# Splitting the last 512-column matrix product ahead of a run of 256-column ones into two halves (two transformer blocks, one Trainium2 core)

## The chip, the cores and the metric

The kernel runs on one core of one Trainium2 chip. The metric is the device time of one execution in microseconds (us). A matrix product here is one TensorE instruction pair: a weight load, which puts a 128x128 stationary operand into the array, and a product, which streams 256 or 512 columns of a second operand past it and adds into a bank of PSUM.

## The reference

Two transformer blocks in sequence on 256 tokens of width 1024, all in float32. Cut to what matters here:

```python
# first block (context tokens feed only the mixer's state)
h = modulate(rmsnorm(x, g0), sh1, sc1)
x = x + g1 * hgrn2_mixer(hc, h, hg_w_in, ...)       # q, f_fwd, f_bwd, i, g = h @ w_in ; ... @ hg_w_out
u = dwconv(modulate(rmsnorm(x, g1_), sh2, sc2) @ ffn_w_up, conv_w, conv_b)   # 1024 -> 2*2816
gate, val = split(u); x = x + g2 * ((silu(gate) * val) @ ffn_w_down)         # 2816 -> 1024
x = rmsnorm(x, final_g)
# second block
proj = rmsnorm(x, pre_mix_norm) @ w_in               # retention, windowed attention, two gates
merged = sigmoid(gate_r) * (ret @ w_ret_out) + sigmoid(gate_s) * (swa @ w_swa_out)
x = x + rmsnorm(merged @ w_out, post_mix_norm)
u = square(relu(rmsnorm(x, pre_mlp_norm) @ w_up))    # 1024 -> 4096
x = x + rmsnorm(u @ w_down, post_mlp_norm)           # 4096 -> 1024
```

## The kernel before

Every large matrix product is taken as three. Each float32 operand is split into a high part (rounded to the type that TensorE streams in one pass) and a low rest, and `mm3` adds high*high, high*low and low*high into one PSUM bank: line 345, 346 and 347, in this order. The weights come from memory in halves of 128x1024 (512 KB) and are split on the core into tiles `hi` (ScalarE, line 157) and `lo` (VectorE, line 158). The activations stand in `hT` (high and low part, transposed, the contraction on the partitions).

The products come in two widths, and the kernel alternates between them.

- **256 columns, into `x` (or `m`) banks.** `fm_product` takes one chunk of 256 output features. The weight slice is loaded as the stationary operand, and 256 tokens of `hT` stream past it: 2 feature halves x 8 contraction steps x 3 = 48 products. In a row of the trace such a product reads `x<-hT,hi` or `x<-hT,lo`: out, then what streams, then what is loaded.
- **512 columns, into `m` banks.** `row_product` multiplies the activations of 256 features back to 1024 output columns. Here the activation is loaded (`ah`, `al`: its high and low part) and 512 columns of weight stream past: `m<-hi,ah`, `m<-lo,ah`, `m<-hi,al`. Its function `go(j)` issues 2 contraction steps x 2 token halves x 2 column halves x 3 = 24 products, into four banks `acc[0..3]` that are kept open over all j.

`row_product` is used four times: for `o1` (the mixer's output, n = 4 chunks), `dn` (the first block's down projection, n = 11), `o2` (the second mixer's output, n = 4) and `d2` (the second down projection, n = 16). `go(j)` covers the first n - SKEW chunks (SKEW = 3), one between two groups of `fm_product`; `finish` takes the last three chunks in another order, one bank after the other. In the first block's feed-forward stage a period is two `fm_product` (gate and value, 96 products) and one `go`; in the second's it is one `fm_product` (48 products) and one `go`.

Other shapes that the prediction reads: the value projection of the first mixer (`v_half`) has the roles turned, weights stream and `hT` is loaded (`m<-hi,hT`, 256 columns); the products with `w_swa_out` stream the split attention output `swh`, `swl` (`x<-swh,hi`, 24 products in a row); `mm3_rows` (lines 331, 335, 336) loads `hT` and streams weights. The start of the program has products of 512 columns with `hT` streaming (`f0_mm`, into four banks `zf`), and the query chunk's 256-column products follow them.

The order on each engine is written out in the kernel; nothing is scheduled by a compiler, and TensorE takes its instructions in that order.

Of the kernel before, what the change touches and what calls it, by code (L numbers as in the profile page):

```python
# [17 lines left out]
KT = 8  # L18
# [12 lines left out]
SKEW = 3  # L31
# [21 lines left out]
def kernel(ctx: ExitStack, tc: tile.TileContext, a, out):  # L53
    nc = tc.nc
    v_, s_, g_, t_ = nc.vector, nc.scalar, nc.gpsimd, nc.tensor
# [8 lines left out]
    def bank(tag):  # L64
        return ps.tile([128, 512], F32, tag=tag, name=tag, bufs=4)
# [103 lines left out]
    def use(i, keep=None, ahead=None):  # L169

        assert i == at_["u"], (i, at_["u"])
        at_["u"] += 1
        at_["rel"] = chunks[i if keep is None else keep][0]
        a0, a1 = chunks[i]
        pump(len(halves) if ahead is None else a1 + ahead)
        assert at_["s"] >= a1
        w = []
        for j in range(a0, a1):
            r = ready.pop(j)
            for k in range(halves[j][1] if r else 0):  # L180
                w.append((r[0][:, k, :], None if r[1] is None else r[1][:, k, :]))
        return w
# [5 lines left out]
    def part_done(i):  # L188

        at_["rel"] = max(at_["rel"], chunks[i][0] + 1)  # L190
        pump(len(halves))
# [103 lines left out]
    start = ctx.enter_context(ExitStack())  # L295
# [43 lines left out]
        for k in range(KT - n, KT):  # L339
            lo(k)  # L340

    def mm3(o, w, x, start, stop):
        wh, wl = w
        xh, xl = x
        t_.matmul(o, wh, xh, start=start, stop=False)  # L345
        t_.matmul(o, wh, xl, start=False, stop=False)  # L346
        t_.matmul(o, wl, xh, start=False, stop=stop)  # L347

    oTs = res.tile([128, 4, 512], F32, name="oTs")

# [8 lines left out]
    def hT(k, c0, c1):  # L359
        return hTh[:, k, c0:c1], hTl[:, k, c0:c1]  # L360
# [3 lines left out]
    def tick(n=1):  # L364
        for _ in range(n):
            if side:
                side.pop(0)()
# [8 lines left out]
    def fm_product(chunk, nk=KT, x=None, tag="x", ticks=0):  # L376

        w = use(chunk)
        z = bank(tag)
        x = x or (lambda k: hT(k, 0, T))  # L380
        for i in range(2):
            c = slice(i * 128, i * 128 + 128)
            for k in range(nk):
                mm3(z[:, i * T:(i + 1) * T], (w[k][0][:, c], w[k][1][:, c]), x(k), k == 0, k == nk - 1)
                if i and nk == KT and k == KT // 2 - 1:
                    part_done(chunk)
                if ticks and k % 4 == 3:
                    tick(ticks)
        return z
# [45 lines left out]
    def f0_mm(w, k, es):  # L435
        wh, wl = w[0]
        for e in es:
            c = slice(e * 128, e * 128 + 128)
            mm3(zf[e], (wh[:, c], wl[:, c]), hT(k, 0, 512), k == 0, k == KT - 1)

    rs, hs, ar = {}, {}, {}
    cs = const.tile([128, 16], F32, name="cs")
# [25 lines left out]
    for k in range(KT):  # L468
# [5 lines left out]
        if k % 2:  # L474
            v_.tensor_add(sq[k], sq[k - 1], sq[k])
            for i in range(4):
                t_.matmul(sb[:, i * 128:(i + 1) * 128], sq[k][:, i * 128:(i + 1) * 128], ones, start=False,
                          stop=k == KT - 1 and i == 3)
# [13 lines left out]
    for i in range(4):  # L492
        t_.matmul(rb[i // 2][:, i % 2 * 128:i % 2 * 128 + 128], r[:, i:i + 1].to_broadcast([128, 128]), ident,
                  start=True, stop=True)
# [7 lines left out]
    zf = [bank("m") for _ in range(4)]  # L502
# [3 lines left out]
    for k in range(KT):  # L506
        w = use(C["f0", k], ahead=0)
        if k:
            f0_mm(w, k, (0,))
        else:  # L510
            wh, wl = w[0]
            c = [slice(e * 128, e * 128 + 128) for e in range(4)]
            for e in range(4):
                t_.matmul(zf[e], wh[:, c[e]], hTh[:, 0, :], start=True, stop=False)
                t_.matmul(zf[e], wl[:, c[e]], hTh[:, 0, :], start=False, stop=False)
# [11 lines left out]
        if k == 0:  # L527
            nc.scalar.dma_start(hmask, a["hmask"])
            for e in range(4):
                t_.matmul(zf[e], wh[:, c[e]], hTl[:, 0, :], start=False, stop=False)  # L530
        else:
            f0_mm(w, k, (1, 2, 3))
# [201 lines left out]
    for p in range(4):  # L734
# [6 lines left out]
        if p == 0:  # L741
            for e in range(4):
                sigmoid_of(e, zf[e])
        else:
            for d in range(2):
                i = C["ff" if d == 0 else "fb", p]
                w = use(i)
                for hh in range(2):
                    z = bank("m")
                    c = slice(hh * 128, hh * 128 + 128)  # L750
                    for k in range(KT):
                        mm3(z, (w[k][0][:, c], w[k][1][:, c]), hT(k, 0, 512), k == 0, k == KT - 1)
                        if hh and k == 3:
                            part_done(i)
                        if d and k % 4 == 3:
                            tick(2)
                    sigmoid_of(2 * d + hh, z)
                for _ in range(1 + d if p < 3 else 2 * d):
                    ada_step()
# [8 lines left out]
        for d in range(2):  # L768
            kk_[d] = yk.tile([128, 2, 2, T], F32, tag="k", name="k")
            for hh in range(2):  # L770
                e = 2 * d + hh
# [101 lines left out]
        while any(live):  # L873
# [4 lines left out]
            if nstep in v_steps[p]:  # L878
                half = v_steps[p].index(nstep)
# [16 lines left out]
    def splits_to(i):  # L896
        at_["cap"] = i
        pump(len(halves))
# [33 lines left out]
    def row_product(name, n, lhs, done):  # L932

        acc = []

        def mms(j, w, kk, tok, half):
            c = slice(half * 512, half * 512 + 512)
            mm3(acc[2 * tok + half], lhs(j, kk, tok), (w[kk][0][:, c], w[kk][1][:, c]),  # L940
                j == 0 and kk == 0, j == n - 1 and kk == 1)

        def go(j, ticks=0):
            if not acc:
                acc.extend(bank("m") for _ in range(4))
            w = use(C[name, j])
            for kk in range(2):
                for tok in range(2):
                    for half in range(2):
                        mms(j, w, kk, tok, half)  # L950
                    tick(ticks)
                if kk == 0:
                    part_done(C[name, j])

        def finish(*limits, caps=()):
            tail = range(n - SKEW, n)
            w = {}
            for j in tail:
                w[j] = use(C[name, j], keep=C[name, n - SKEW])
                for kk in range(2):  # L960
                    for half in range(2):
                        mms(j, w[j], kk, 0, half)
            d0, d1 = done(0, acc[0:2]), done(1, acc[2:4])
            for i in range(4):
                f0 = next(d0)
                if caps:
                    splits_to(caps[i])
            for j in tail:
                for kk in range(2):
                    mms(j, w[j], kk, 1, 0)  # L970
            next(d1)
            for j in tail:
                if f0 and j == n - 1 - bool(caps):
                    f0()
                    at_["cap"] = 1 << 30
                    pump(limits[0])
                for kk in range(2):
                    mms(j, w[j], kk, 1, 1)
                    at_["rel"] = chunks[C[name, j]][0] + kk + 1
            for limit in limits[1:]:  # L980
                pump(limit, True)
            for _ in limits[1:]:
                next(d1)
                if held:
                    held.pop(0)()
            while held:
                held.pop(0)()
            return [x for x in d1][-1]
        return go, finish
# [231 lines left out]
    w = {}  # L1221
    for tok in range(2):
        for j in range(2):
# [5 lines left out]
            def done(k):  # L1229
                if tok and k % 2:  # L1230
                    at_["rel"] = chunks[C["vr", j, 0]][0] + k // 2 + 1
                    pump(len(halves))
# [325 lines left out]
```

## Time and profile before

| | |
|---|---|
| device time, median of 3 runs | 861.56 us (860.24 to 861.66) |
| device time of the profiled execution | 861.0 us |
| its span in the trace | 859.2 us |
| TensorE busy (products) | 845.5 us, 98% of the span, 6270 products |
| VectorE busy | 603.3 us, 70% |
| ScalarE busy | 488.7 us, 57% |
| mean granted TensorE clock | 0.996 |
| DMA | 161.89 MB, mean 188 GB/s |

The profiled execution's own time is 1.8 us more than its span: what lies ahead of the first and behind the last instruction. A product's row in the trace has a start and a duration. Products overlap, so the duration (0.28 us for 256 columns) is not what one costs; the cost in a run of products is the distance from one start to the next.

### The profile page before, as it was taken

What the parts mean: (1) busy time and instruction counts of PE and PEld (TensorE: products, weight loads), DVE (VectorE), ACT (ScalarE), POOL (GpSimd) and SP (SyncE); (2) the same over time, 40 slices, a digit from 0 to 9 for tenths busy, and PEclk for the clock granted to TensorE, in tenths of its full rate; (3) what the DMA queues carried; (4) which work ended last, traced back from release to release, by engine and by line L of the source; (5) the groups of instructions that cost most, each with busy time, mean ns of one, the idle gap of its engine ahead of it and who ended that gap; (6) DMA issues with size and microseconds to landing.
All of it is one profiled execution on the core that took longest, in us unless ns stands there. A gap on an engine that the chain in (4) does not pass through costs nothing.

```text
span 859.2 us, 15573 instructions
## 1 busy us (share of the span) xinstructions
PE 845.5 (98%) x6270; PEld 773.4 (90%) x6270; DVE 603.3 (70%) x979; ACT 488.7 (57%) x797; POOL 17.1 (2%) x27
## 2 busy tenths in 40 slices
PE   8999999999999999999999999999999999999997
PEld 7798988989987999999988899999999899999995
DVE  5768869877978689887778556665576786555532
ACT  4586575758765575664555546765643674444431
POOL 0000000000000000000000000000000000000000
PEclk9999999999999999999999999999999999999999
DMA  9981735728255667867754654545795188666401
GB/s 350 391 275 49 240 130 158 258 75 269 81 165 184 234 221 243 273 216 223 247 152 99 203 170 145 150 124 172 215 304 169 37 306 253 188 187 189 142 1 49
DMA packets 115784, 161.89 MB, mean 188 GB/s; under 512 B 13952, under 2 KB 95744, under 8 KB 115712
## 3 DMA queue, kind: packets, MB, share of 16 engines
q1 hardware_dynamic: 113408, 155.80, 56.1%
q10 hardware_dynamic: 2304, 5.10, 1.8%
q8 instruction: 49, 0.80, 0.4%
q14 instruction: 23, 0.19, 0.1%
HBM read 159.83 MB, written 1.05 MB: 187 GB/s over the span
## 4 chain that ended last, share of the span: by engine, by line
PE 82%; DVE 9%; ACT 4%; DMA 2%; issue 2%; POOL 0%; POOLq 0%; DVEq 0%; ACTq 0%
PE m L345 15%; PE m L346 15%; PE m L347 15%; PE x L345 8%; PE x L346 8%; PE x L347 8%; DVE lo L158 2%; PE x L712 1%; ACT hi L157 1%; PE x L405 1%; PE x L335 1%; DMA raw<-in_hg_w_in_dram 1%; PE x L336 1%; ACT sig L779 1%; ACT k L774 1%
## 5 line engine op out<-in xcount | busy, mean ns | idle before, releaser
L158 DVE TENSOR_TENSOR lo<-raw,hi 128x1024 fp32r<-128x1024 f32 (+1 forms) x248 | 291.1, 1204 | 127.5 <-ACT hi L157 123.5
L157 ACT ACTIVATE hi<-raw 128x1024 fp32r<-128x1024 f32 (+1 forms) x248 | 249.7, 1040 | 120.4 <-PE x L346 47.6
L345 PE MATMUL m<-hT,hi 128*128 128x256 f32 (+1 forms) x556 | 174.8, 314 | 0.0
L347 PE MATMUL m<-hT,lo 128*128 128x256 f32 (+1 forms) x556 | 168.6, 303 | 0.0
L346 PE MATMUL m<-hT,hi 128*128 128x256 f32 (+1 forms) x556 | 168.5, 303 | 0.0
L345 PE MATMUL x<-hT,hi 128*128 128x256 f32 x592 | 166.4, 281 | 0.0
L346 PE MATMUL x<-hT,hi 128*128 128x256 f32 x592 | 165.7, 280 | 0.0
L347 PE MATMUL x<-hT,lo 128*128 128x256 f32 x592 | 165.7, 280 | 0.0
L345 PEld LDWEIGHTS m<-hT,hi 128*128 128x128 f32 x556 | 104.5, 188 | 9.5 <-issue 4.4
L347 PEld LDWEIGHTS x<-hT,lo 128*128 128x128 f32 x592 | 113.0, 191 | 0.0
L345 PEld LDWEIGHTS x<-hT,hi 128*128 128x128 f32 x592 | 111.3, 188 | 1.0 <-ACT hi L157 0.2
L346 PEld LDWEIGHTS x<-hT,hi 128*128 128x128 f32 x592 | 111.1, 188 | 1.0 <-issue 0.2
L346 PEld LDWEIGHTS m<-hT,hi 128*128 128x128 f32 x556 | 104.6, 188 | 5.4 <-DVE hT L433 0.7
L347 PEld LDWEIGHTS m<-hT,lo 128*128 128x128 f32 x556 | 104.3, 188 | 5.1
L345 PE MATMUL m<-hi,ah 128*128 128x512 f32 x248 | 96.7, 390 | 0.0
L347 PE MATMUL m<-hi,al 128*128 128x512 f32 x248 | 96.6, 390 | 0.0
L346 PE MATMUL m<-lo,ah 128*128 128x512 f32 x248 | 96.5, 389 | 0.0
L347 PEld LDWEIGHTS m<-hi,al 128*128 128x128 f32 x248 | 46.6, 188 | 9.9 <-DVE al L1198 0.2
L346 PEld LDWEIGHTS m<-lo,ah 128*128 128x128 f32 x248 | 46.6, 188 | 8.7
L345 PEld LDWEIGHTS m<-hi,ah 128*128 128x128 f32 x248 | 46.6, 188 | 8.6
L591 DVE SCALAR_TENSOR_TENSOR vr<-raw,cs,vr 128x1024 f32<-128x1024 f32 x28 | 35.8, 1280 | 0.4
L345 PE MATMUL m<-hi,hT 128*128 128x256 f32 x128 | 35.8, 280 | 0.0
(314 smaller groups left out, 1237.2 us busy)
## 6 DMA issues: line engine op xcount, KB each, us to landing
raw<-in_ffn_w_up_dram SPq DMA_DIRECT2D x44, 512.0 KB, 5.2
raw<-in_w_in_dram SPq DMA_DIRECT2D x42, 512.0 KB, 4.1
raw<-in_hg_w_in_dram SPq DMA_DIRECT2D x36, 512.0 KB, 5.2
raw<-in_w_ada_dram SPq DMA_DIRECT2D x32, 512.0 KB, 5.6
raw<-in_w_up_dram SPq DMA_DIRECT2D x32, 512.0 KB, 4.8
raw<-in_w_down_dram SPq DMA_DIRECT2D x32, 512.0 KB, 3.7
raw<-in_ffn_w_down_dram SPq DMA_DIRECT2D x22, 512.0 KB, 4.4
ar<-in_ada_dram SPq DMA_DIRECT2D x16, 512.0 KB, 7.7
```

The source lines that it names most:

```text
L157: s_.activation(h[:, :w], r[:, :w], AF.Copy)
L158: held.append(lambda r=r, h=h, l=l, w=w: v_.tensor_tensor(l[:, :w], r[:, :w], h[:, :w].bitcast(F32), op=OP.subtract))
L335: t_.matmul(o, hTh[:, k, c], w[k][0], start=k == 0, stop=False)
L336: t_.matmul(o, hTh[:, k, c], w[k][1], start=False, stop=False)
L345: t_.matmul(o, wh, xh, start=start, stop=False)
L346: t_.matmul(o, wh, xl, start=False, stop=False)
L347: t_.matmul(o, wl, xh, start=False, stop=stop)
L405: t_.matmul(rw[g, :256], c2[:, kk, :], ar[k][kk // 4][:, kk % 4, :], start=kk < 4, stop=kk >= 4)
L591: v_.scalar_tensor_tensor(acc, w[kk][0], cs[:, k:k + 1], acc, op0=OP.mult, op1=OP.add)
L712: t_.matmul(z[:, b * 128:(b + 1) * 128], l, r, start=i == 0, stop=i == len(terms) - 1)
L774: s_.activation(kk_[d][:, :, hh, :], sig[e], AF.Identity, scale=noml[:, ix:ix + 1], bias=oml[:, ix:ix + 1])
L779: s_.activation(sig[e], sig[e], AF.Ln, scale=oml[:, ix:ix + 1], bias=lb[:, ix:ix + 1])
```

## The change

`mm3` gets a flag. Where it is set, the third product (low part loaded, high part streamed) is issued as two products of 256 columns, into the two halves of the same bank, each with its own load of the same stationary operand. The flag is set for the last product of `f0_mm` and, in `row_product`, for the last product of every `go(j)` and for the last product of `finish`.

```diff
-    def mm3(o, w, x, start, stop):
+    def mm3(o, w, x, start, stop, halved=False):
+
+
         wh, wl = w
         xh, xl = x
         t_.matmul(o, wh, xh, start=start, stop=False)
         t_.matmul(o, wh, xl, start=False, stop=False)
-        t_.matmul(o, wl, xh, start=False, stop=stop)
+        if halved:
+            t_.matmul(o[:, 0:256], wl, xh[:, 0:256], start=False, stop=False)
+            t_.matmul(o[:, 256:512], wl, xh[:, 256:512], start=False, stop=stop)
+        else:
+            t_.matmul(o, wl, xh, start=False, stop=stop)
...
-            mm3(zf[e], (wh[:, c], wl[:, c]), hT(k, 0, 512), k == 0, k == KT - 1)
+            mm3(zf[e], (wh[:, c], wl[:, c]), hT(k, 0, 512), k == 0, k == KT - 1, e == 3 and k == KT - 1)
...
             mm3(acc[2 * tok + half], lhs(j, kk, tok), (w[kk][0][:, c], w[kk][1][:, c]),
-                j == 0 and kk == 0, j == n - 1 and kk == 1)
+                j == 0 and kk == 0, j == n - 1 and kk == 1,
+                kk and tok and half and (j < n - SKEW or j == n - 1))
```

TensorE then has 28 more products: one at `f0`, two at `o1`, nine at `dn`, two at `o2` and fourteen at `d2`. The other engines' instructions stay in number and order. Behind 20 of the 28 places a run of `fm_product` with `hT` streaming follows at once (7 at `dn`, 1 at `o2`, 12 at `d2`). Behind the others stand the query chunk (`f0`), transposes or `mm3_rows` (`o1`, and `finish` of `o2`), products of 512 columns (the last `go` and `finish` of `dn`, the last `go` of `d2`), and the end of the program (`finish` of `d2`).

On TensorE, the end of one `go` of `d2` and the start of the next `fm_product` stood like this before the change (numbers are line numbers of the kernel before):

```order
L346 MATMUL m<-lo,ah 128x512
L347 MATMUL m<-hi,al 128x512
L345 MATMUL m<-hi,ah 128x512
L346 MATMUL m<-lo,ah 128x512
L347 MATMUL m<-hi,al 128x512
L345 MATMUL x<-hT,hi 128x256
L346 MATMUL x<-hT,hi 128x256
```

The same place with the change (its line numbers are those of the changed kernel, where 347, 348, 353 are the three products and 350, 351 the two halves):

```order
L348 MATMUL m<-lo,ah 128x512
L353 MATMUL m<-hi,al 128x512
L347 MATMUL m<-hi,ah 128x512
L348 MATMUL m<-lo,ah 128x512
L350 MATMUL m<-hi,al 128x256
L351 MATMUL m<-hi,al 128x256
L347 MATMUL x<-hT,hi 128x256
L348 MATMUL x<-hT,hi 128x256
```

The step from 512 to 256 columns now falls one product earlier, within the `m<-hi,al` products, and the step from `hi` streaming to `hT` streaming falls between two products of 256 columns.

At the end of `f0` on TensorE, ahead of the query chunk, `hT` streams on both sides of the step, with the change:

```order
L347 MATMUL m<-hT,hi 128x512
L348 MATMUL m<-hT,hi 128x512
L350 MATMUL m<-hT,lo 128x256
L351 MATMUL m<-hT,lo 128x256
L347 MATMUL m<-hT,hi 128x256
```

Only the width changes there, one product earlier than before; what streams and what is loaded stay of one kind.

## Rows read from the trace of the kernel before

**Rows 1.** The profile's page: span, and shares of the chain that ended last.

```profile
span 859.2 us, 15573 instructions
...
PE 82%; DVE 9%; ACT 4%; DMA 2%; issue 2%; POOL 0%; POOLq 0%; DVEq 0%; ACTq 0%
```

**Rows 2.** Windows, all engines: stretch, length; busy us and count by engine; clock; DMA.

```profile
core 0: us, PE busy (x) PEld busy (x) DVE busy (x) ACT busy (x) POOL busy (x), PEclk, DMA share, GB/s
368.44:385.19 16.75, 16.75 (x121) 15.81 (x120) 12.90 (x18) 10.91 (x14) 0.00 (x0) 1.00 0.68 220
781.15:792.24 11.09, 11.09 (x73) 10.16 (x72) 6.10 (x7) 5.25 (x6) 0.00 (x0) 1.00 0.60 189
```

**Rows 3.** Timeline of TensorE where a go ends: start, duration, instruction.

```profile
703.27 0.39 PE L347 MATMUL m<-hi,al 128*128 128x512 f32 x1
703.50 0.28 PE L345 MATMUL x<-hT,hi 128*128 128x256 f32 x1
703.61 0.28 PE L346 MATMUL x<-hT,hi 128*128 128x256 f32 x1
703.73 0.28 PE L347 MATMUL x<-hT,lo 128*128 128x256 f32 x1
```

**Rows 4.** Windows, TensorE's products with hT: length, busy (count), clock, DMA.

```profile
core 0: us, PE busy (x), PEclk, DMA share, GB/s
296.54:312.75 16.21, 16.21 (x144) 1.00 0.50 158
318.20:329.51 11.31, 11.31 (x96) 1.00 0.80 266
418.68:429.99 11.31, 11.31 (x96) 1.00 0.72 234
638.36:644.02 5.66, 5.66 (x48) 1.00 0.74 228
703.50:709.15 5.65, 5.65 (x48) 1.00 0.61 195
825.52:831.18 5.66, 5.66 (x48) 1.00 0.00 0
```

**Rows 5.** Windows, TensorE: two runs of go, of 24 products each.

```profile
698.04:703.50 5.46, 5.46 (x27) 1.00 0.89 326
709.15:714.59 5.44, 5.44 (x26) 1.00 0.89 276
```

**Rows 6.** Timeline of TensorE where the swh products end.

```profile
646.77 0.28 PE L347 MATMUL x<-swh,lo 128*128 128x256 f32 x1
646.89 0.29 PE L345 MATMUL x<-hT,hi 128*128 128x256 f32 x1
647.01 0.28 PE L346 MATMUL x<-hT,hi 128*128 128x256 f32 x1
647.13 0.28 PE L347 MATMUL x<-hT,lo 128*128 128x256 f32 x1
647.25 0.28 PE L345 MATMUL x<-hT,hi 128*128 128x256 f32 x1
647.36 0.28 PE L346 MATMUL x<-hT,hi 128*128 128x256 f32 x1
```

**Rows 7.** Windows, TensorE's products with hT, behind two runs of swh products.

```profile
624.94:630.03 5.09, 5.09 (x47) 1.00 1.04 372
647.25:652.35 5.10, 5.10 (x47) 1.00 0.55 166
```

**Rows 8.** Windows, TensorE: 21 products of a run with swh and swl.

```profile
644.37:646.89 2.52, 2.52 (x24) 1.00 0.74 222
```

**Rows 9.** Windows, products with hT: the query chunk behind f0, then v_half.

```profile
49.23:54.89 5.66, 5.66 (x49) 1.00 0.80 252
55.36:60.80 5.44, 5.44 (x51) 1.00 0.94 315
```

**Rows 10.** Windows, products with hT: mm3_rows behind finish of o1 and of o2.

```profile
272.35:277.88 5.53, 5.53 (x47) 1.00 0.32 96
672.46:677.79 5.33, 5.33 (x47) 1.00 0.00 0
```

**Rows 11.** Timeline of TensorE behind the first mm3_rows: [idle before <-releaser].

```profile
280.75 0.44 PE L1013 MATMUL x<-ident,ep 128*128 128x128 f32 x2 [2.59 <-DVE ep L1043]
```

## The prediction

> **What bounds the kernel now.** The page's chain first: 82% of it is TensorE [rows 1]. The change touches TensorE alone, so the question is whether TensorE is the bound where the change acts. The windows of one period of each feed-forward stage say yes: of 16.75 us and of 11.09 us TensorE is busy all the time at a granted clock of 1.00 (its upper level, 2.4 GHz), while VectorE is busy 12.90 and 6.10 us, ScalarE 10.91 and 5.25 us, and the DMA engines 68% and 60% [rows 2]. A nanosecond off TensorE's stream there is one off the end, until some 20% have gone.
>
> Next, what a product costs there, from starts and not from durations. A go has 24 products of 512 columns: 5.44 us, 227 ns each [rows 5]. Behind it the products of 256 columns come at 0.11 to 0.12 us from the first one on [rows 3], and the windows resolve it: 96 in 11.31 us, 48 in 5.65 us, which is **117.8 ns** each [rows 4]. The reader should set beside this the first row of that group: the same function, the same shape, also with hT streaming, but behind transposes and not behind a go: 143 products (a window also counts the one to three products that began ahead of it and still drain; this one counts 144) in 16.21 us, **113.4 ns** each, at the same clock. And a third spacing: the products with swh take 2.52 us for 21, **120.0 ns** each [rows 8]. So one shape has three spacings, at full clock, with no wait named in between, and each holds to the end of its series. A series' spacing is set by how it is entered. I call them close (113), wide (118) and widest (120). The rows don't tell what in the engine remembers it.
>
> How many series are wide: behind the go of dn seven of 96 products, the first and the last of them in [rows 4] (318.20, 418.68), both 11.31 us; behind the go of o2 one of 48 (638.36); behind the go of d2 twelve of 48, first and last at 703.50 and 825.52. Those are the 20 places where the change puts its halves ahead of fm_product.
>
> **The change part by part.**
>
> *The halves.* 28 times one product of 227 ns becomes two of 256 columns. At the wide spacing a pair is 235.6 ns, 9 ns more: 28 x 9 = 0.25 us. Bounds: at the close spacing twice 113.4 is 227, nothing; at the widest 240 ns, 0.37 us. I take 0.25, since a series entered from a go is wide from its first product [rows 3]. No wait is added: both halves go to a bank that is open anyway. The last pair (end of d2) adds its 9 ns to the tail, the pair at o1's finish stands ahead of a series behind which TensorE waits 2.59 us for VectorE anyway [rows 11], so it costs nothing; both are inside the 0.25.
>
> *The entry into the series of 256.* Now the width, what streams and what is loaded all change at one step. With the change the width changes first, among products that stream hi, and then the operands change between two products of 256 columns. The trace has that second step elsewhere: from 256 columns of swh to 256 columns of hT. There four starts take 0.47 us (646.89 to 647.36) [rows 6], and then the series is close: 45 products in 5.10 us, 113.3 ns each, and the same behind the swh series before it, 5.09 us [rows 7]. Another change of operands at 256 columns, from the wide query chunk (48 products in 5.66 us) to v_half, also ends in the close spacing (48 products in 5.44 us) [rows 9]. So wherever the operands change between products of 256 columns and hT is streamed or loaded next, the spacing behind is close; I know three such places and they agree. If it holds at the 20 places:
> - at dn a series goes from 11.31 to 96 x 113.3 = 10.88 us: 0.43 x 7 = 3.0 us;
> - at o2 and d2 from 5.65 to 5.44 us: 0.21 x 13 = 2.7 us;
> - the entry itself: 0.47 us against 4 x 113.3 = 0.453, 0.02 us each, 0.4 us in all (bounds: nothing, if the halves have taken it already; 0.4);
> - the next go: behind a close series it took 5.46 us, behind a wide one 5.44 [rows 5], 0.02 x 20 = 0.4 us (bounds 0 and 0.4).
>
> Gain 5.7, cost 0.25 + 0.4 + 0.4 = 1.05, net **4.7 us**.
>
> *The other places.* At f0 hT streams on both sides and only the width changes; nothing there resembles the swh step, so I leave the query chunk wide (if it went close: 5.66 to 5.44, 0.2 us). Behind finish of o1 mm3_rows is wide (47 in 5.53 us), but TensorE waits behind it [rows 10, 11], so a closer series would only wait longer. Behind finish of o2 it is close already, 47 in 5.33 us [rows 10]: nothing to win. That last one is also a warning: it is a step from 512 columns straight into a close series, so the step of width alone doesn't make a series wide.
>
> *Sum.* 861.0 us (the profiled execution's own time) - 4.7 = 856.3. The median of the runs is 0.56 higher, which would make 856.9; I forecast **856.5 us**.
>
> **The rivals.**
>
> *No change of spacing (time 861.8).* The first half of a 512-column product streams what the new half streams, with the same operand loaded next, and the go runs at its steady 227 ns. Then the halves may run at 113.4 as that half does, and hT's first product meets TensorE exactly as it does today, and the series is wide. For it: today all 20 series behind a go come out wide, whatever buffers they use, so what a go leaves behind is very regular. Against it: swh's series at the widest spacing streams the same way as the halves would (a split operand against a split weight), and it does not stay with TensorE when hT follows. Price: the halves alone, 861.56 + 0.25 = 861.8, between 861.4 and 862.2 with the bounds and the runs' spread. The same time comes out if a product of a shape simply has one price and the spacings of [rows 4] have causes elsewhere, such as the operands' places. The Trainium skill, "TensorE: Matmul & The Clock Gate", section "Back-to-back issue gap", gives such a price: N/2.4 + 2.5 ns for an isolated product, 109 ns at 256 columns and 216 at 512, with which the 28 pairs would cost an estimated 0.07 us and no series would change. The trace does not agree with it: at a clock of 1.00 the shape costs 113, 118 or 120 ns.
>
> *Only one of the two stages changes (time 859).* The series of dn are 96 long and those of d2 48, with other buffers loaded. Only dn: 3.0 less 0.25 and about a third of 0.8, 2.5 us; only o2 and d2: 2.7 - 0.25 - 0.5 = 1.9 us. So 858.5 to 859.7. Against it: today they behave alike.
>
> *The halves bring on the widest spacing (time 864.5; the other side).* If two halves start the 120.0 ns of the swh series, and hT's series behind keeps it, 7 x 96 + 13 x 48 = 1296 products cost 2.2 ns more: 2.9 us, with 0.25 for the halves 861.56 + 3.1 = 864.7. It decides the sign alone, and is measurable once more than half of these series keep that spacing. For it: the swh series keep it for 21 products [rows 8]. Against it: no series with hT in the trace does; both that follow swh leave it within three products.
>
> *Another engine takes over.* Close series would shorten dn's period to 16.35 us against 12.90 of VectorE, and d2's to 10.9 against 6.10; the DMA share rises from 68% to 70%. It would need one of them to be at its end, and none is [rows 2]. I give it nothing of its own.
>
> **How the numbers follow.** All or nearly all 20 series close: 0.62. One stage only: 0.06. No change of spacing: 0.26. Widest spacing: 0.06. The forecast is the first case's; its own range, with all costs at nothing (861.0 - 5.7 = 855.3) and all at their upper bounds from the highest of the three times (861.66 - 5.7 + 1.2 = 857.2), is 855.2 to 857.3. To leave out no more than 2 in 10 the range has to reach the case without a change, up to 862.0; below I add 0.2 for the query chunk: 855.0 to 862.0. What this kernel's runs can tell from no change is about 0.2%, 1.7 us. Faster than that: the first two cases, 0.67. Within it: 0.27. Slower: 0.06.
>
> **What would show it right or wrong.** In the changed kernel's windows: the series behind each go of dn at 10.9 us and of d2 at 5.44 to 5.46 (right), 11.3 and 5.65 (no change of spacing), 11.5 and 5.76 (widest). The two halves: starts 0.23 to 0.24 us over the pair. The go behind a close series: 5.46 us. The first three products of hT behind the halves at 0.12 and then 0.113. TensorE still busy through the whole period; if gaps appear in it, with VectorE or a DMA named as what ended them, the bound has moved. The forecast is wrong in its main step if the series stay at 117.8 though the operands now change at 256 columns; then what the three agreeing places share is something else than that.

## The result and the profile after

The changed kernel takes **854.64 us** (854.23 to 854.88, 4 runs) against 861.61 us (860.24 to 861.69, 4 runs): ratio **0.9927**, interval 0.9913 to 0.9941. The forecast was 856.5, with a range of 855.0 to 862.0: faster, as forecast, and by 7.0 us (0.7%) where the sum said 4.7. The time itself lies 0.4 us below the lower end of the range. The profiled execution took 854.23 us.

The page of the changed kernel, its first lines and its chain, beside [rows 1]:

```profile
span 852.4 us, 15630 instructions
...
PE 839.3 (98%) x6298; PEld 767.6 (90%) x6298; DVE 603.1 (71%) x979; ACT 489.2 (57%) x797; POOL 17.1 (2%) x27
...
PE 87%; DVE 6%; ACT 3%; DMA 2%; issue 1%; POOL 0%; SPq 0%; POOLq 0%; DVEq 0%; ACTq 0%
```

28 products more, and TensorE is busy 6.2 us less (845.5 before). Nothing took its place: its share of the chain rose. Windows over one period of `dn` and one of `d2`, all engines (columns as in [rows 2]):

```profile
360.18:376.54 16.36, 16.36 (x123) 15.45 (x122) 13.68 (x21) 9.13 (x12) 0.00 (x0) 1.00 0.78 265
780.68:791.60 10.92, 10.92 (x75) 10.01 (x74) 6.10 (x7) 5.26 (x6) 0.00 (x0) 1.00 0.69 202
```

The periods were 16.75 and 11.09 us. TensorE fills the new ones too. Windows on the series of `hT` behind the go of `dn` (first and last), of `o2`, and of `d2` (first and last), which answer to [rows 4]:

```profile
316.57:327.46 10.89, 10.89 (x96) 1.00 0.80 273
414.73:425.62 10.89, 10.89 (x96) 1.00 0.75 251
633.84:639.30 5.46, 5.46 (x48) 1.00 0.69 207
698.78:704.24 5.46, 5.46 (x48) 1.00 0.59 193
818.90:824.36 5.46, 5.46 (x48) 1.00 0.02 3
```

The other 15 take 10.89 to 10.90 and 5.46 us in the same trace: all 20 series are close. Windows on a go of `d2` with its pair of halves, the first and the second, beside [rows 5]: 

```profile
693.32:698.78 5.46, 5.46 (x27) 1.00 0.87 319
704.24:709.70 5.46, 5.46 (x27) 1.00 0.90 264
```

The timeline of TensorE at the end of that first go, which answers to [rows 3] and reads like [rows 6]:

```profile
698.33 0.39 PE L348 MATMUL m<-lo,ah 128*128 128x512 f32 x1
698.55 0.28 PE L350 MATMUL m<-hi,al 128*128 128x256 f32 x1
698.66 0.28 PE L351 MATMUL m<-hi,al 128*128 128x256 f32 x1
698.78 0.29 PE L347 MATMUL x<-hT,hi 128*128 128x256 f32 x1
698.90 0.28 PE L348 MATMUL x<-hT,hi 128*128 128x256 f32 x1
699.03 0.28 PE L353 MATMUL x<-hT,lo 128*128 128x256 f32 x1
699.14 0.28 PE L347 MATMUL x<-hT,hi 128*128 128x256 f32 x1
```

The pair takes 0.23 us, the first four steps of `hT` 0.48 us (the fifth product starts at 699.26), and from there on the products come at 0.113.

**Where the 6.8 us of span went**, from the starts of the same products in both traces: 0.1 us up to o1's wait at 278 us; **1.5** between there and 296 us; **2.7** over the seven periods of `dn`; 0.4 in the series behind the last go of `dn`, 0.2 of which is given back up to 490 us; 0.2 at `o2`; **2.1** at `d2`. What the sum priced is 2.7 + 0.2 + 2.1 = 5.0. The other 1.5 us lies where the change does nothing: these are windows on TensorE there, first before, then after:

```profile
281.60:296.20 14.60, 14.23 (x110) 0.88 0.65 227
```

```profile
281.60:296.20 14.60, 14.23 (x123) 1.00 0.72 246
```

Before, the granted clock stood below its upper level (2.4 GHz) for some microseconds, right behind the 2.59 us in which TensorE waits for VectorE [rows 11]; products of 256 columns came there at 0.21 us (282.71, 282.92, 283.13). After, the same wait (2.57 us) is followed by a clock of 1.00. Two questions for experiments: is it the break that makes the series close, and does the 1.5 us belong to the change?

### The profile page after: what moved, and what is told of

Its sections match the earlier page's. It is cut to its first block, busy times and chain, and to the rows that moved or that the text cites. A ratio compares the mean times of both kernels' runs of the same rounds, so it can differ in the third digit from the quotient of the medians.

```text
span 852.4 us, 15630 instructions
## 1 busy us (share of the span) xinstructions
PE 839.3 (98%) x6298; PEld 767.6 (90%) x6298; DVE 603.1 (71%) x979; ACT 489.2 (57%) x797; POOL 17.1 (2%) x27
## 4 chain that ended last, share of the span: by engine, by line
PE 87%; DVE 6%; ACT 3%; DMA 2%; issue 1%; POOL 0%; SPq 0%; POOLq 0%; DVEq 0%; ACTq 0%
PE m L347 17%; PE m L348 16%; PE m L353 16%; PE x L353 8%; PE x L347 8%; PE x L348 8%; PE x L718 2%; DVE lo L158 2%; DMA ar<-in_ada_dram 1%; DMA xT<-in_xcT_dram 1%; PE x L648 1%; ACT hi L157 1%; PE x L335 1%; PE x L411 1%; PE x L336 1%
## 5 line engine op out<-in xcount | busy, mean ns | idle before, releaser
L158 DVE TENSOR_TENSOR lo<-raw,hi 128x1024 fp32r<-128x1024 f32 (+1 forms) x248 | 291.0, 1203 | 121.2 <-ACT hi L157 118.9
L347 PE MATMUL x<-hT,hi 128*128 128x256 f32 x592 | 164.3, 278 | 0.0
L348 PE MATMUL x<-hT,hi 128*128 128x256 f32 x592 | 163.6, 276 | 0.0
L353 PE MATMUL x<-hT,lo 128*128 128x256 f32 x592 | 163.5, 276 | 0.0
L353 PEld LDWEIGHTS x<-hT,lo 128*128 128x128 f32 x592 | 111.2, 188 | 0.0
L353 PE MATMUL m<-hi,al 128*128 128x512 f32 x223 | 87.0, 390 | 0.0
L353 PEld LDWEIGHTS m<-hi,al 128*128 128x128 f32 x223 | 41.9, 188 | 9.2 <-DVE al L1205 0.4
```

Source lines behind the costliest of these rows:

```text
L158: held.append(lambda r=r, h=h, l=l, w=w: v_.tensor_tensor(l[:, :w], r[:, :w], h[:, :w].bitcast(F32), op=OP.subtract))
```

## The experiments

Diffs are against the changed kernel unless the text says otherwise. The times of the kernel before that stand beside a run were taken on the same chip as that run.

**1. The halves six products earlier.** 23 go have the broken product as the one that is followed by six of 512 columns; `f0` and the `finish` calls have none.

```diff
-                kk and tok and half and (j < n - SKEW or j == n - 1))
+                kk and not tok and half and j < n - SKEW)
```

> The halves stand six products earlier: in each of the 23 go it is the low*high product of the first token half, second column half, second contraction step, and six products of 512 columns follow it, so that hT follows 512 columns as in the kernel before. Theory (the spacing behind a go is reset because the operands change between two products of 256 columns): the series behind stay wide, 11.31 us per 96 and 5.65 us per 48, and the time is that of before plus 23 x 6 to 9 ns, 861.7 to 861.9 us. Rival (any pair of halves near the end of a go disturbs a regular pattern, and that is enough): the series are close, 10.9 and 5.45 us, and the time is near 857 us.

861.89 us, one execution; before on this chip 861.1 (13 executions, 859.59 to 862.11). Windows on the series of `dn` and `d2`:

```profile
318.14:329.45 11.31, 11.30 (x96) 1.00 0.75 252
704.00:709.65 5.65, 5.65 (x48) 1.00 0.65 199
```

All 20 are wide. A break anywhere near the end of the go is not enough.

**2. Three products earlier.**

```diff
-                kk and tok and half and (j < n - SKEW or j == n - 1))
+                kk and tok and not half and j < n - SKEW)
```

> The halves stand three products earlier: the low*high product of the second token half, first column half, second contraction step of each of the 23 go, with three products of 512 columns behind it. In the trace before, the first products of 512 columns behind a change took 231 to 236 ns and settled to 227 after three to five. Theory (the operands have to change between products of 256 columns): the series stay wide, 861.7 to 861.9 us. Rival (what counts is whether the products just ahead of hT are at their settled 227 ns or still disturbed, as they were ahead of the close series behind finish of o2): the three products behind the halves are at 230 ns or more and the series are close, near 857 us.

862.84 us, one execution. The timeline of TensorE, then a window on the series of `dn` behind it:

```profile
316.83 0.28 PE L350 MATMUL m<-hi,al 128*128 128x256 f32 x1
316.94 0.28 PE L351 MATMUL m<-hi,al 128*128 128x256 f32 x1
317.06 0.40 PE L347 MATMUL m<-hi,ah 128*128 128x512 f32 x1
317.30 0.40 PE L348 MATMUL m<-lo,ah 128*128 128x512 f32 x1
317.53 0.39 PE L353 MATMUL m<-hi,al 128*128 128x512 f32 x1
317.76 0.28 PE L347 MATMUL x<-hT,hi 128*128 128x256 f32 x1
```

```profile
317.76:329.06 11.30, 11.30 (x96) 1.00 0.77 254
```

The first two products of 512 behind the halves take 0.235 us each instead of 0.227, so the go is not at rest when `hT` comes, and yet the series is wide: 96 in 11.30 us. That a disturbed stream is what counts falls. A go with its halves takes 5.51 us here on the mean of 19, against 5.44 before, which is some 1.5 us over 23 go. Another 0.7 us of the loss (862.84 against 861.1) may have nothing to do with the halves: the 156 products of 256 columns with `hT` behind 489 us, in a stretch that no edit touches, take 18.38 us in this trace and 17.70 in that of the kernel before.

**3 and 4. One stage alone.** In experiment 3 the flag is set in `dn` alone (nine places; this is the diff shown), in experiment 4 in `o2` and `d2` (16 places).

```diff
-                kk and tok and half and (j < n - SKEW or j == n - 1))
+                name == "dn" and kk and tok and half and (j < n - SKEW or j == n - 1))
```

> The halves at dn alone, 9 of the 28 places. By the changed kernel's trace a period of dn is 16.36 us against 16.75, seven of them. Theory: -2.7 us, with the halves' cost at the two other places +0.01. If the 1.5 us that the trace gained between 282 and 296 us (a fallen clock in the trace before, none in the one after) comes with the change at o1, it is missing here: 858.9 us. If it is chance from run to run, the time is 858.9 or 857.4 with the granted clock of each run telling which.

> The halves at o2 and d2 alone, 16 of the 28 places. By the changed kernel's trace a period of d2 is 10.92 us against 11.09, twelve of them, and o2 gains 0.19. Theory: -2.3 us, 859.3 us. All of the code up to 632 us is that of the kernel before, so if the fall of the clock at 282 us belongs to that code it is here too, with a mean granted clock of 0.996; if it is chance, some of these runs have 0.998 and are 1.5 us shorter.

`dn` alone: 858.05 us (856.31 to 858.45, 5 executions), ratio 0.996 (0.9946 to 0.9975). `o2` and `d2` alone: 858.54 (857.15 to 858.97, 9), ratio 0.997 (0.996 to 0.998). Windows on a series of `dn` and one of `d2`, in the kernel with `dn` alone and then in the other:

```profile
317.95:328.85 10.90, 10.90 (x96) 1.00 0.73 245
700.69:706.35 5.66, 5.66 (x48) 1.00 0.64 193
```

```profile
316.33:327.64 11.31, 11.31 (x96) 1.00 0.79 260
701.74:707.20 5.46, 5.46 (x48) 1.00 0.64 202
```

Each part turns its own series and leaves those of the other part as they were, and each pays. At a like mean clock `dn` brings 3.0 to 3.2 us (858.2 against 861.2 at 0.997, 856.4 against 859.6 at 0.999) and the other part 2.4 to 2.5 (857.2 against 859.6, 858.7 at 0.996 against 861.2); one of its nine executions, 858.54 us at 0.999, does not fit this split. The 0.4 us that `dn` has over the 2.7 stands behind its last go, whose last product is broken too. There `hT` does not follow at once: two products of 512 columns with `ones` (the trace counts them as four, 1.3 us) stand between. That series of `hT` took 11.71 us before (436.76 to 448.47) and takes 11.30 with `dn` alone (433.79 to 445.09) and with the whole change; it stays at 11.71 in experiment 6, where this one product is whole and the seven before it are broken. Windows on it, with the whole change and in experiment 6:

```profile
432.40:443.70 11.30, 11.30 (x96) 1.00 0.62 182
```

```profile
433.73:445.44 11.71, 11.71 (x96) 1.00 0.59 174
```

So the broken product need not stand right ahead of `hT`.

**5 and 6. The changed kernel again, and only the 20 places in front of a series.** Experiment 6 drops the eight places behind which the diff puts no series:

```diff
-                kk and tok and half and (j < n - SKEW or j == n - 1))
+                kk and tok and half and name != "o1" and j < n - SKEW - (name in ("dn", "d2")))
```

> The changed kernel once more, for how often the granted clock falls behind the wait at 278 to 281 us. In the 13 executions of the kernel before on this chip 11 had a mean clock of 0.997 and about 861.2 us, two 0.999 and 859.6. If the fall is chance, some executions of the changed kernel have it too: 856.2 us at 0.996 to 0.997 and 854.6 at 0.998 to 0.999, and like against like the change is worth 5.0 us. If the change itself keeps the clock up, all executions are near 854.6.

> The halves only at the 20 places ahead of fm_product; left whole again at f0, at both places of o1, at the last go and finish of dn, at finish of o2 and at the last go and finish of d2. In the changed kernel's trace a pair takes 113 + 119 ns against 227, 5 to 6 ns more, so the eight others cost 0.05 us, and finish of o2 had turned the series behind it from close to wide (0.2 us, ahead of a wait). Theory: the gain is all at the 20 places; 854.5 to 854.7 us at the same clock, not to be told from the changed kernel. Rival (one of the eight does something, such as f0 or o1 keeping the clock up): 856 us.

On this chip: before 861.0 (859.33 to 862.08, 17 executions); the change again 854.97 (854.27 to 856.08, 5), ratio 0.9934 (0.9922 to 0.9946); the 20 places 855.96 (854.5 to 857.09, 6), ratio 0.994 (0.9928 to 0.9951). The 20 places have two executions at 854.5, like the change, and four at a lower mean clock between 855.9 and 857.1. The same split runs through before: five of its 17 executions here take 859.3 to 859.8 us, at a mean clock of 0.999; the other twelve take 860.4 to 862.1, eleven of them at 0.996 to 0.998. And one execution of the unaltered change, too, took 856.08 at 0.996. Another execution of the change, 855.79 us at 1.000, is not explained by the clock. So by the mean clocks the fall comes with each of the kernels, in before's more often than not, and the traces agree: over 281 to 283 us the clock is 0.50 with the 20 places and 1.00 in experiment 4, which leaves everything up to 632 us as it was before. The median of the 20 places is the number that I had put down for the rival, but its four longer executions have the lower clock and its two others take what the change takes. The medians therefore can't tell the eight places apart from nothing.

**7 and 8. The wait behind o1 filled.** Nine products of constants into an unused bank go in where TensorE waits, in the kernel before (7) and in the changed kernel (8); nothing reads what they write. The trace counts them as 18.

```diff
+                    if n == 3:
+                        fz = bank("m")
+                        for _ in range(9):
+                            t_.matmul(fz[:, 0:128], ones, ones, start=True, stop=True)
```

> The kernel before, with nine products of 128x128 constants into a free bank put into TensorE's wait of 2.6 us at 278 us; their result is not used. They take about 2 us, less than the wait. If the 1.5 us between 282 and 296 us is the clock that falls behind this wait, all executions are at 859.6 us with 0.999; if the wait has nothing to do with it, most stay at 861.2 with 0.997; if the products are longer than the wait, the time grows by the difference.

> The changed kernel with the same nine products in the wait. Theory: 854.5 us in all executions, and against the kernel before with the products 5.0 us less, which is the change alone with the clock taken out of the comparison.

Timeline of TensorE, filled kernel before, which answers to [rows 11], and the windows there:

```profile
277.69 2.17 PE L1112 MATMUL m<-ones 128*128 128x128 f32 x18
280.41 1.09 PE L1013 MATMUL x<-ident,ep 128*128 128x128 f32 x8 [0.55 <-DVE ep L1043]
281.26 0.36 PE L335 MATMUL x<-hi,hT 128*128 128x256 f32 x1
281.46 0.28 PE L336 MATMUL x<-lo,hT 128*128 128x256 f32 x1
```

```profile
281.60:296.20 14.60, 14.23 (x123) 1.00 0.78 265
```

Before, filled: **859.41** us (859.22 to 859.88, 11 executions), ratio 0.9985 (0.9976 to 0.9993). After, filled: **854.62** (854.29 to 854.91, 5), ratio 0.9927 (0.9915 to 0.9939). With the wait filled no execution of either shows a time or a mean clock of the fall, and before's spread shrinks from 2.8 us to 0.7. Before gains 1.6 us by it, after only 0.35 against its median on this chip. The change by itself is 859.41 - 854.62 = **4.8 us**.

**9 and 10. Broken, but not in halves.** The 28 last products as 128 and 384 columns, then as 384 and 128.

```diff
-            t_.matmul(o[:, 0:256], wl, xh[:, 0:256], start=False, stop=False)
-            t_.matmul(o[:, 256:512], wl, xh[:, 256:512], start=False, stop=stop)
+            t_.matmul(o[:, 0:128], wl, xh[:, 0:128], start=False, stop=False)
+            t_.matmul(o[:, 128:512], wl, xh[:, 128:512], start=False, stop=stop)
```

> As the change, but the product is taken as 128 + 384 columns in place of 256 + 256, at all 28 places: there is a break, but the product just ahead of hT is longer than 256. Theory (the product ahead of hT has to be as short as hT's own): the series behind stay wide, 117.8 ns. Rival (any break of that product in two is enough): close, 113.4 ns. The pair costs about 111 + 170 ns against 227, 55 ns more, 1.5 us in all: 862.7 us if wide, 857.9 if close, at the usual clock of the kernel before.

> The 28 last products are taken as 384 and then 128 columns. If any break of that product into two parts right ahead of hT's products is enough, the 20 series behind it are at 113.3 ns a product, and the time is that of the 128 + 384 kernel, 857 to 858.5 us with the clock fallen behind the 2.6 us wait and 1.5 us less without. If the first part has to be short (at most 256 columns, so that the operand is loaded again at least 109 ns behind the last load), the series stay at 117.8 ns and the time is 861.5 to 863 us, before's with 28 pairs that cost 10 to 60 ns more each. The pair itself: starts 0.23 to 0.29 us over it, as the 286 ns of 128 + 384.

128 + 384: 857.84 us, one execution, before there 861.6. 384 + 128: 855.65, one execution, before there 860.45. The timeline of 128 + 384:

```profile
318.08 0.22 PE L350 MATMUL m<-hi,al 128*128 128x128 f32 x1
318.14 0.39 PE L351 MATMUL m<-hi,al 128*128 128x384 f32 x1
318.37 0.28 PE L347 MATMUL x<-hT,hi 128*128 128x256 f32 x1
318.49 0.28 PE L348 MATMUL x<-hT,hi 128*128 128x256 f32 x1
```

A window on its series of `dn`:

```profile
318.37:329.27 10.90, 10.90 (x96) 1.00 0.80 259
```

With 384 + 128, the first two products of `hT` and a window on the series:

```profile
316.76 0.33 PE L347 MATMUL x<-hT,hi 128*128 128x256 f32 x1
316.93 0.28 PE L348 MATMUL x<-hT,hi 128*128 128x256 f32 x1
```

```profile
316.76:327.72 10.96, 10.96 (x96) 1.00 0.79 257
```

Both are close, with a dearer entry: the pair of 128 + 384 takes 0.29 us, and behind 384 + 128 the first step of `hT` takes 0.17. This fells what I had expected of the first of the two, that the product ahead must be no wider than `hT`'s. At the 20 places its width does not decide; that the go's last product comes in two does. Every cut also loads the same operand twice, and no run separates this second load from the shorter product. Behind the last go of `dn`, where the two products with `ones` stand between, the cuts differ: 11.31 us for 384 + 128 (433.02 to 444.33), but 11.70, wide, for 128 + 384 (434.63 to 446.33).

**11 and 12. The place of `hT`** (against the kernel before). The buffer of `hT` from o1 on is moved by 64 bytes (11); the places of `hT` in the first mixer and from o1 on are swapped, 128 bytes apart (12).

```diff
-    hTh, hTl = h_at(0)
+    hTh, hTl = h_at(16)
```

> The kernel before with no halves, and with hT moved by 64 bytes in its tile from the o1 stage on, so that its rows start at odd multiples of 64 bytes as those of hi, lo, swh and swl do (before, hT's start at multiples of 128 bytes). Asked: whether the spacings hang on the operands' places. If they do, hT's series should act as the swh series, at 120.0 ns whatever stands ahead: some 1900 products of 256 columns with hT streaming behind 296 us go from 113.4 or 117.8 to 120.0, and the time rises by 5 to 9 us, to 866 to 870. If places mean nothing, all spacings and the time (861) stay.

> The kernel before with hT's two places swapped: in its tile hT stands 128 bytes into it up to the g products and at its start from the o1 stage on; here the other way round. Asked: whether the first mixer's series of 256 columns, of which most are wide in the trace before (49.2, 100.8, 150.9, 214.8 and 225.9 us, some 200 products), and those behind (mostly close where nothing of 512 columns stands ahead) differ by the place. If a move by 128 bytes matters, the wide ones of the mixer become close (0.9 us less) and the close ones behind become wide; if only the parity at 64 bytes matters, nothing changes: 861 us.

Moved by 64 bytes: 872.25 us; swapped: 868.56; before there 861.6; one execution each. Windows on a series of `dn` and one of `d2` with the 64 bytes, then, swapped, on a series of `dn` and on the one behind transposes at 298 us:

```profile
319.41:330.93 11.52, 11.52 (x96) 1.00 0.78 253
713.24:718.99 5.75, 5.75 (x48) 1.00 0.69 203
```

```profile
320.50:331.81 11.31, 11.31 (x96) 1.00 0.79 253
297.98:315.02 17.04, 17.04 (x144) 1.00 0.52 171
```

In these two traces there is no close series behind a go nor behind the transposes: 119.9 ns a product with the 64 bytes, 117.8 swapped (17.04 us with its first step; before, the same stretch takes 16.42), where the series behind transposes has 113.4 in [rows 4]. Both sizes were missed. For the 64 bytes I had counted 1900 products; 2688 of 256 columns stream `hT` behind 290 us in the trace before, and their steps take 4.0 ns more on the mean (121.2 against 117.3), which is the 10.6 us. Swapped, the wide series of the mixer did not become close either. So the place of `hT` moves the spacings; with before's place both spacings occur, and there the break changed the series from one to the other. Whether a break helps at another place was not run.

## Why the prediction was right, and where it was not

**The bound** was read rightly: both periods shortened by what TensorE's stream lost, 0.39 and 0.17 us, and no wait took the place.

**The series** were sized rightly. `dn`: forecast 2.7 net of its costs, measured 2.7. `o2` and `d2`: forecast 2.1 net, measured 2.3. All 20 became close, which rules out no change of spacing, one stage only, and the widest spacing.

**The small costs**: the halves cost 5 ns (0.232 against 0.227 us) where I took 9; the entry 0.02 us and the next go 5.46 us, both as forecast.

**The net** was 4.7; with the clock held up by the filler it is 4.8. **The missing 2 us** of the comparison, which put the time below the range, are mostly the clock behind o1's wait (1.5 us): my sum started from an execution that had the fall and had no term for it, though its trace showed it, a clock of 0.77 over 281.60 to 289.00. The range reached down only to what the series and the costs could give from that start. I had taken that wait for a place where nothing can be won, and hadn't read the stretch behind it. What the runs show is that the fall isn't the change's doing, as it comes and goes from execution to execution in both. The changed kernel has it less often, in one of nine executions by the mean clock (0.996), but these are few, and why is open.

**The other places**: the query chunk and `mm3_rows` of o1 stayed wide, as forecast. `mm3_rows` behind finish of `o2` went from close to wide: 5.33 us in [rows 10], now, in a window,

```profile
667.62:673.16 5.54, 5.54 (x50) 1.00 0.00 0
```

(it begins one product early, at the second half), which I had not forecast; a wait behind it hides it (from the `finish` products to the first go of `d2` both traces take 42.8 us). This is no accident of one trace: it is wide in all six traces in which the last product of `finish` at `o2` is broken, and close in the six others with `hT` in its place. There `hT` is loaded and not streamed, and the break does the opposite of what it does at the 20 places. And the sum had no gain for the last go of `dn`; the series of `hT` behind it became close, 0.4 us, of which the `finish` behind it gives 0.2 to 0.3 back.

**The reason given for the main step was wrong, though its forecast held.** That the size came out right on such a reason was luck in part. I had said that a change of operands between two products of 256 columns brings the close spacing, from three places that agreed. Two things speak against it. 128 + 384 gives close series without such a step. And the third place, [rows 9], does not hold: in the kernel of experiment 3, which has the kernel before's instructions there, the query chunk was close and v_half behind it wide. Windows on the two:

```profile
49.57:55.01 5.44, 5.44 (x50) 1.00 0.79 256
55.01:60.66 5.65, 5.65 (x50) 1.00 0.92 298
```

So a change of operands can end a close series as well as start one. Nor is a spacing set by the entry of its series alone, as I had written: the place of `hT` sets it too (experiments 11 and 12). The same instructions on the same chip also gave a wide query chunk, in experiment 1 (5.65 us, 49.51 to 55.16). The query chunk is not the only series that switches with no edit near it: the 156 products of 256 columns with `hT` behind 485 us take 17.70 us in the changed kernel's first trace and 18.38 in that of experiment 5, the same kernel.

What stands after twelve runs: behind a go, a last product in two parts made the series of `hT` close at all 20 places, at each of three cuts and on every chip that these runs fell on. With as many halves three or six products earlier, or with none, all 20 were wide. In every one of the fourteen traces the series that were treated alike came out alike, so chance does not explain them, and the number of products and loads in a go does not either. It is no rule for `hT` at large: the query chunk stands right behind a broken product of `f0` and was wide with it, and `mm3_rows` behind `o2` went from close to wide. Windows on the query chunk, with the change:

```profile
49.49:55.15 5.66, 5.66 (x51) 1.00 0.80 248
```

What in TensorE that acts on is open. In all three cuts the entry costs something extra (steps of 0.12 and 0.13 us behind the halves, a pair of 0.29 at 128 + 384, a step of 0.17 at 384 + 128) and the series then runs at 0.113; whether that loss is the cause, or only goes with it, no run here tells. The Trainium skill, "TensorE: Matmul & The Clock Gate", section "Back-to-back issue gap", says that in a stream of loads and products the spacing is set by both together. No run here changes the load alone, so none shows it. Its price by columns alone, for an isolated product, does not describe these series: in experiments 11 and 12 the place of one operand moved the same shape from 113 to 118 or 120 ns.

## What to carry to other kernels

Measure what a product costs by starts over a whole run of like products, and compare runs of the same shape: one that is 4% dearer at full clock may be something to win. Here breaking the product ahead of it won it; the two moves of an operand in memory that were tried lost 7 and 11 us. Test either on the kernel at hand and look at every series behind it, as the break turned one close series wide here. Before a difference of under 1% is put down to a change, look whether the granted clock is the same behind every wait in both traces, and whether the series that the change does not touch kept their spacing (0.7 us in one series here).

## What was not expected of the hardware

- A shape has several spacings at a granted clock of 1.00 (113, 118 and 120 ns for 256 columns), and moving a streamed operand by 64 bytes costs 1.2% of the kernel (872.25 against 861.6 us).
- A wait of 2.6 us is followed by a fall of the granted clock in some executions and not in others: the stretch from 272 to 296 us takes 23.7 to 24.0 us in six traces with the fall and 22.4 in four without, with `hT` in its place and the wait as it was; with 2.2 us of work on constants in it, none of 16 executions of the two kernels shows such a time.
- The same instructions at the same places showed other spacings in other executions ([rows 9] against experiment 3; 5.65 against 5.44 us for the query chunk on one chip; 17.70 against 18.38 us in one and the same kernel), while the 20 series behind broken products were close in every trace.
